# Two instead of four gate tiles inside attention, the six-head run of pooling tiles, and VectorE work queued behind the negated maxima

## The chip, the cores and the metric

The kernel is one program on one core of a Trainium2 chip. The metric is the device time of one execution in microseconds. The engines are named as the profile names them: PE is TensorE (matrix products), with PEld its weight loads; DVE is VectorE, ACT is ScalarE, POOL is GpSimd, SP is SyncE, which here only starts transfers.

## The reference

One decoder layer on 512 tokens of width 1024, in float32:

```python
proj = h @ w_in                       # q | k | v | pool_in | gate_logits
q, k, v, p, g = split(proj)           # 512, 512, 512, 512, 2048 columns
y_attn = moba_attention(q, k, v, rel_bias) @ w_branch_attn   # 8 heads of 64, causal softmax with a bias by distance
y_pool = multiscale_pool(p, w_pool_group, pool_scale) @ w_branch_pool
gates = sigmoid(g).reshape(B, S, 2, D)
mixed = gates[:, :, 0] * y_attn + gates[:, :, 1] * y_pool
h = layer_norm(ALPHA * h + mixed @ w_out)
a, u = split(h @ w_ffn_in)
f = (gelu(causal_dwconv(a)) * u) @ w_ffn_out
h = layer_norm(ALPHA * h + f)
```

With 512 tokens and blocks of 256 the three selected blocks are all the past ones, so attention is plain causal attention. Each head is 512 by 512 scores, of which the lower triangle of 128-wide blocks is computed.

## The kernel before, in words

**Float32 by three products.** A float32 operand is split into a rounded part `hi` and a remainder `lo` (`split`, L71 to L77: ACT writes `hi`, DVE subtracts to get `lo`). A product is three matmuls: hi·hi, hi·lo, lo·hi (`mm3`, lines 243, 246, 247). Every weight slab of 128x1024 thus costs one ACT and one DVE instruction, and sits in a ring of five slots (`slot`); raw slabs land in three buffers (`wraw`, the A slabs of the seven-product form too). `weights(i)` fetches up to `LEAD` = 3 slabs ahead, but not past `state["limit"]`.

**Two ways to make a pair of tiles.** A tile of 128 output channels by 512 tokens and 1024 input channels is either direct (`in_tile`: 8 x 3 matmuls of 512 columns), or two such tiles are made together by a Strassen-like scheme of seven products (`seven`: 7 x 4 x 3 matmuls of 256 columns), with four weight slabs named A, X, D, Y and four forms of the activations (`nT1`, `T3`, `nT2`, `T4`), which `t_form` builds on DVE from the four quarters of x (`quads`) and splits.

**Stages around the change.** First v, the pooling inputs and q and k are made. Then the heads run in a loop of eight. Head h gets its operands by `head` (ACT and DVE cut k and q into parts, and SP copies them to the other half of the partitions: tiles k1, kl, q1), its scores by `scores` (PE; then four DVE instructions that add the bias and take the maxima, `pp` and `nm`; DVE negates the maxima; ACT takes the exponentials with their sums `rs`; DVE inverts; POOL normalizes in four pieces), its transposes by `trans` (ten on PE into three banks `tr`; ACT copies one, DVE two, to `PT`), and two heads at a time their product with v by `pv` (tile `ob`, ACT copies it to `oT`). `head` and `scores` run two heads ahead. As PE's filler between these steps stand tiles that depend on no head: four direct gate tiles (`g0`, `g8`, `g1`, `g9`) in iterations 0 to 3, and in 4 to 7 four pooling tiles `br f, 1` (f = 0 to 3; 4 x 3 matmuls of 512 columns from `zT`, one slab per two tiles), copied by DVE to `gates` (`early_branch`). The four splits of `zT` stand one in each of iterations 0 to 3.

Behind attention come ten more branch tiles (`br 4,1`, `5,1`, `6,1`, and `br f, 0` from `oT` for f = 6 and 0 to 5) with the four forms for the gates between them, and then the gate pairs f = 2 to 7 by `seven` (`sag`, `sbg`, `scg`), the last branch tiles, the output projection (`wo`) and the feed-forward part.

**What sets the order.** The program is recorded in the order of the Python code; a scheduler then puts the instructions of each engine in a fixed order by its own estimated times, and an engine runs its list strictly in that order, waiting at the head of it. `with tc.issue_after(ins):` keeps what is recorded in the block behind `ins` on `ins`'s engine. The output projection and the feed-forward part are the same before and after.

Of the kernel before, what the change touches and what calls it, by code (L numbers as in the profile page):

```python
# [8 lines left out]
F32 = mybir.dt.float32  # L9
# [5 lines left out]
P = 128  # L15
S = 512
# [3 lines left out]
H = 8  # L20
# [18 lines left out]
RAW = 1  # L39
KH = NF // 2  # L40
TAIL = 8
GSEVEN = 2
BRANCH = (("z", 0), ("z", 1), ("z", 2), ("br", 6), ("o", 0), ("o", 1), ("o", 2), ("br", 7))
SEVEN = tuple(range(2, 19))
COVER = 4
# [7 lines left out]
def layer_kernel(ctx: ExitStack, tc: tile.TileContext, xT, x, w_v, w_c, rel_bias, invcnt, w_group,  # L53
                 pscale, w_br, w_out, lnr, w_fi, convp, w_fo, out):
    nc = tc.nc
# [9 lines left out]
    def bank(name):  # L65
        return ps.tile([P, S], F32, tag="ps", name=name)

    def flip(v):
        (pst, pn), (_, n) = v.ap
        return bass.AP(tensor=v.tensor, offset=v.offset + P - 1, ap=[[pst, pn], [P, n // P], [-1, P]])  # L70

    def split(hi, lo, src, copy=None):
        if copy:
            copy(hi, src)
        else:
            state["hi"] = nc.scalar.activation(hi, src, AF.Copy)  # L76
        state["lo"] = nc.vector.tensor_tensor(lo, src, hi.bitcast(F32), op=ALU.subtract)  # L77
        return state["lo"]
# [5 lines left out]
    at = {}  # L84
    pair_of = {}

    def add(key, *tiles):
        at[key] = len(chunks)
        chunks.extend(tiles)

    def add_seven(key, *two):
        pair_of[key] = two
        for q in "AXDY":
            add((*key, q), (key, q))
# [4 lines left out]
    for p in range(pairs):  # L99
        add_seven(("i", 1 + p), w_c[first["q"] + p], w_c[first["k"] + p])  # L100
    fill = [("g", 8 * g + f) for f in range(GSEVEN) for g in range(2)]
    for n, j in fill:
        add((n, j), w_c[first[n] + j])
    for n, key in enumerate(BRANCH[:-1]):
        add(key, w_br[n])
    for f in range(GSEVEN, KT):
        add_seven(("g", f), w_c[first["g"] + f], w_c[first["g"] + KT + f])
    add(BRANCH[-1], w_br[len(BRANCH) - 1])
    WO0 = len(chunks)
# [18 lines left out]
    state = {"next": 0, "limit": WO0 - 1}  # L128
# [107 lines left out]
    def weights(i):  # L236
        while state["next"] <= min(i + LEAD, state["limit"]):
            fetch()
        return ready[i]
# [76 lines left out]
    zT = keepp.enter_context(tc.tile_pool(name="keepz", bufs=1)).tile([P, 4, S], F32, name="zT")  # L316
# [174 lines left out]
    def in_tile(kind, j):  # L491
        wh, wl = split3(weights(at[kind, j]), KT)
        b = bank(f"{kind}{j}")
        for kt in range(KT):
            mm3(b, (wh[:, kt, :], wl[:, kt, :]), (xT_hi[:, kt, :], xT_lo[:, kt, :]), kt == 0, kt == KT - 1)
        if kind == "p":
            return b
        else:
            gslot[j] = gates[:, len(gslot), :]
            nc.scalar.activation(gslot[j], b, AF.Copy)  # L500
# [34 lines left out]
    nms = {}  # L535
    exps = {}
# [65 lines left out]
            scores(0)  # L602
    phase.close()
    keep = keepp.enter_context(tc.tile_pool(name="keep", bufs=1, reuse_waits="tile"))
    gates = keep.tile([P, 2 * GSEVEN + 4, S], F32, name="gates")
    oT = keep.tile([P, 4, S], F32, name="oT")
    zT_hi = keep.tile([P, 4, S], F32R, name="zT_hi")
    zT_lo = keep.tile([P, 4, S], F32R, name="zT_lo")
# [4 lines left out]
    def trans(h):  # L613
        pp = Ps[h]
        PT = ap.tile([P, 10 * P], F32, tag="PT", name=f"PT{h}")
        bk = [bank(f"tr{h}_{n}") for n in range(3)]
        for kb in (0, 1, 3, 2):
            o = toff[kb]
            for i in range(kb, NT):
                c = o + (i - kb) * P  # L620
                nc.tensor.transpose(bk[c // S][:, c % S:c % S + P], pp[:, offs[i] + kb * P:offs[i] + (kb + 1) * P],
                                    ident)
        nc.scalar.activation(PT[:, :S], flip(bk[0]), AF.Copy)
        nc.vector.tensor_copy(PT[:, S:2 * S], flip(bk[1]))
        state["PT"] = nc.vector.tensor_copy(PT[:, 2 * S:], flip(bk[2][:, :2 * P]))
        PTs[h] = PT

    def pv(p):
        b = bank(f"ob{p}")
        for kb in range(NT):  # L630
            n = (NT - kb) * P
            for e in range(2):
                h = 2 * p + e
                state["pv"] = nc.tensor.matmul(b[e * DH:(e + 1) * DH, kb * P:], vv[:, kb, h * DH:(h + 1) * DH],
                                 PTs[h][:, toff[kb]:toff[kb] + n], start=kb == 0, stop=kb == NT - 1)
        state["o"] = nc.scalar.activation(oT[:, p, :], b, AF.Copy)
# [3 lines left out]
    def br_mm(f, br, b=None, ks=range(4), pin=False):  # L640
        key, o = (("br", f), 4 * br) if f >= 6 else (("oz"[br], f // 2), f % 2 * 4)
        wh, wl = split3(weights(at[key]), KT)
        b = b or bank(f"br{f}_{br}")
        for k in ks:
            src = (zT_hi[:, k, :], zT_lo[:, k, :]) if br else (oT_hi[:, k, :], oT_lo[:, k, :])
            mm3(b, (wh[:, o + k, :], wl[:, o + k, :]), src, k == 0, k == 3, pin and k == ks[0])
        return b

    def early_branch(f):
        t = branch[f, 1] = gates[:, 2 * GSEVEN + f, :]  # L650
        nc.vector.tensor_copy(t, br_mm(f, 1))
# [4 lines left out]
    for h in range(H):  # L656
        if h + 2 < H:
            head(h + 2, nms[h], exps[h])
        if h < 4:
            in_tile(*fill.pop(0))  # L660
        elif h < H - 1:
            early_branch(h - 4)
        if h + 2 < H:
            scores(h + 2)
        with ExitStack() as held:
            if h and h % 2 == 0:
                pv(h // 2 - 1)
                held.enter_context(tc.issue_after(state["pv"].ins))
            trans(h)
        if h < 4:  # L670
            with tc.issue_after(nms[h].ins), tc.issue_after(exps[h].ins):
                split(zT_hi[:, h, :], zT_lo[:, h, :], zT[:, h, :])
        if h == 5:
            with tc.issue_after(state["norm"].ins), tc.issue_after(state["dup"].ins):
                for n, (k, t) in enumerate(((k1, t1), (k1, t2), (k2, t1), (k2, t2))):
                    nc.gpsimd.dma_start(quads[n], xT[k.start * P:k.stop * P, t].rearrange("(k p) t -> p k t", p=P))
                homes["g", "X"], homes["g", "D"] = lambda f: gX, lambda f: gD
                for q in "XD":
                    coming[q].remove(("g", GSEVEN))
                    fetch_raw(("g", GSEVEN), q)  # L680
                    homes.pop(("g", q))
        if h == H - 1:
            early_branch(h - 4)
    pv(H // 2 - 1)
    attn.close()

# [4 lines left out]
    more = bp.tile([P, 4, S], F32, name="more")  # L691
# [11 lines left out]
        nc.gpsimd.tensor_tensor(a, b, a, op=ALU.add)  # L703
        mts[f] = a

    unused = [more[:, n, :] for n in range(4)]
    forms = list(parts)
    order = [(4, 1), (5, 1), (6, 1), (6, 0)] + [(f, 0) for f in range(6)]
    for n, (f, br) in enumerate(order):
        if f < GSEVEN:  # L710
            with tc.issue_after(state["o"].ins):
# [35 lines left out]
    for f in range(GSEVEN, KT):  # L747
        if f == KT - 1:
# [3 lines left out]
              lambda ba, u, f=f: gate_done(f, ba, u), first_half if f == KT - 1 else None)  # L752
# [439 lines left out]
```

## Time and profile before

| | |
|---|---|
| time before, median of 3 | 627.69 us (626.48 to 627.84) |
| the profiled execution | 626.34 us, span 624.6 us |
| PE busy | 615.4 us, 99% of the span |
| DVE busy | 513.8 us, 82% |
| ACT busy | 361.6 us, 58% |
| POOL busy | 118.5 us, 19% |
| mean granted PE clock | 0.996 |
| attention loop and branch tiles | about 88 to 181 us of the span |
| gate pairs by seven products | about 181 to 245 us |

Times in rows are microseconds from the start of the span unless marked ns. A busy PE in the profile is not PE at its peak: matmuls are pipelined, so what counts is the distance from one matmul's start to the next one's. In a row of the timeline the second number lasts until the result is written and overlaps the next row.

### The profile page before, as it was taken

The numbers are of one execution on the slowest core, as the hardware profiler recorded it, in microseconds if no ns is written. First come the engines' busy times: TensorE is split into PE (matmuls) and PEld (weight loads), VectorE is DVE, ScalarE is ACT, GpSimd is POOL, SyncE is SP. The second block draws the span as 40 slices with busy tenths as digits, with TensorE's granted clock in tenths as the row PEclk, the third lists the DMA queues.
The fourth block names the chain that finished last, engine by engine and source line by source line (L and its number), as shares of the span: only waits on it lengthen the run. The fifth ranks groups of instructions, "written<-read, shape, count | busy, mean of one in ns | idle before, by whom it ended". The sixth has DMA issues, their size and how long they took to land.

```text
span 624.6 us, 10605 instructions
## 1 busy us (share of the span) xinstructions
PE 615.4 (99%) x4060; PEld 554.8 (89%) x4060; DVE 513.8 (82%) x792; ACT 361.6 (58%) x551; POOL 118.5 (19%) x132
## 2 busy tenths in 40 slices
PE   9999999999999999999999999999999999999995
PEld 6899998786789998889999999999999888888884
DVE  5978788784967988399998988898988959698886
ACT  6746778663756567125566565566656446555452
POOL 0133135344031201110110101101100302123301
PEclk9999999999999999999999999999999999999998
DMA  8566648445486315806658787678744995899805
GB/s 317 165 195 188 172 121 227 124 118 181 123 209 178 103 66 172 301 36 207 164 162 198 200 202 184 176 196 206 186 101 151 331 259 124 204 205 206 204 0 135
DMA packets 41778, 109.29 MB, mean 175 GB/s; under 512 B 4464, under 2 KB 4984, under 8 KB 41472
## 3 DMA queue, kind: packets, MB, share of 16 engines
q1 hardware_dynamic: 27952, 72.55, 34.2%
q0 software_dynamic: 13200, 35.15, 29.3%
q10 hardware_dynamic: 576, 0.92, 0.4%
q8 instruction: 32, 0.52, 0.3%
q14 instruction: 18, 0.15, 0.1%
HBM read 104.39 MB, written 3.17 MB: 172 GB/s over the span
## 4 chain that ended last, share of the span: by engine, by line
PE 97%; DVE 1%; DMA 1%; ACT 0%; POOL 0%; issue 0%; DVEq 0%; POOLq 0%; ACTq 0%
PE saf L243 5%; PE saf L246 5%; PE saf L247 5%; PE v L426 3%; PE fi L243 3%; PE fi L247 3%; PE fi L246 3%; PE sbf L243 3%; PE sbf L247 3%; PE sbf L246 3%; PE wo L246 2%; PE wo L243 2%; PE wo L247 2%; PE br L243 2%; PE br L247 2%; PE br L246 2%
## 5 line engine op out<-in xcount | busy, mean ns | idle before, releaser
L77 DVE TENSOR_TENSOR wlo<-araw,whi 128x1024 fp32r<-128x1024 f32 x56 | 68.1, 1224 | 6.9 <-ACT whi L76 6.4
L76 ACT ACTIVATE whi<-araw 128x1024 fp32r<-128x1024 f32 x56 | 58.7, 1059 | 25.2 <-PE saf L246 5.2
L76 ACT ACTIVATE whi<-wraw 128x1024 fp32r<-128x1024 f32 (+1 forms) x49 | 49.8, 1022 | 35.5 <-DMA wraw<-in_w_fo 8.6
L77 DVE TENSOR_TENSOR wlo<-wraw,whi 128x1024 fp32r<-128x1024 f32 (+1 forms) x49 | 58.4, 1197 | 12.6 <-ACT whi L76 12.4
L76 ACT ACTIVATE whi<-tw 128x1024 fp32r<-128x1024 f32 (+1 forms) x30 | 29.5, 985 | 25.3 <-DMA tw<-in_w_fo 10.5
L190 POOL DMA_DIRECT2D xraw<-in_w_fi x15 | 18.1, 1206 | 134.7 <-DMA xraw<-in_w_fi 74.0
L77 DVE TENSOR_TENSOR wlo<-tw,whi 128x1024 fp32r<-128x1024 f32 (+1 forms) x30 | 33.4, 1129 | 8.5 <-ACT whi L76 8.5
L243 PE MATMUL saf<-hT_hi,whi 128*128 128x256 f32 x136 | 38.0, 279 | 0.0
L243 PE MATMUL sbf<-T_hi,whi 128*128 128x256 f32 x136 | 37.9, 279 | 0.0
L246 PE MATMUL saf<-hT_lo,whi 128*128 128x256 f32 x136 | 37.8, 278 | 0.0
L243 PE MATMUL saf<-nT_hi,whi 128*128 128x256 f32 x136 | 37.8, 278 | 0.0
L247 PE MATMUL saf<-nT_hi,wlo 128*128 128x256 f32 x136 | 37.8, 278 | 0.0
L246 PE MATMUL sbf<-T_lo,whi 128*128 128x256 f32 x136 | 37.7, 278 | 0.0
L247 PE MATMUL sbf<-T_hi,wlo 128*128 128x256 f32 x136 | 37.7, 278 | 0.0
L246 PE MATMUL saf<-nT_lo,whi 128*128 128x256 f32 x136 | 37.7, 277 | 0.0
L247 PE MATMUL saf<-hT_hi,wlo 128*128 128x256 f32 x136 | 37.7, 278 | 0.0
L246 PE MATMUL fi<-hT_lo,whi 128*128 128x256 f32 (+1 forms) x112 | 36.2, 326 | 0.0
L247 PE MATMUL fi<-hT_hi,wlo 128*128 128x256 f32 (+1 forms) x112 | 36.2, 326 | 0.0
L243 PE MATMUL fi<-hT_hi,whi 128*128 128x256 f32 (+1 forms) x112 | 36.1, 327 | 0.0
L566 POOL TENSOR_SCALAR pp<-pp,rs 128x128 f32<-128x128 f32 (+3 forms) x32 | 24.3, 774 | 31.3 <-DVE rs L563 27.8
L231 POOL DMA_DIRECT2D tw<-in_w_fo x18 | 15.6, 901 | 63.0 <-DVE wlo L77 61.4
L243 PEld LDWEIGHTS saf<-hT_hi,whi 128*128 128x128 f32 x136 | 25.5, 188 | 0.1
(356 smaller groups left out, 2207.0 us busy)
## 6 DMA issues: line engine op xcount, KB each, us to landing
tw<-in_w_fo POOLq DMA_DIRECT2D x20, 512.0 KB, 8.6
araw<-in_w_fi SPq DMA_DIRECT2D x17, 512.0 KB, 3.5
xraw<-in_w_fi SPq DMA_DIRECT2D x15, 512.0 KB, 3.9
xraw<-in_w_fi POOLq DMA_DIRECT2D x15, 512.0 KB, 6.5
araw<-in_w_c SPq DMA_DIRECT2D x11, 512.0 KB, 4.1
wraw<-in_w_fi SPq DMA_DIRECT2D x10, 512.0 KB, 3.9
wraw<-in_w_fo SPq DMA_DIRECT2D x10, 512.0 KB, 5.0
tw<-in_w_fo SPq DMA_DIRECT2D x10, 512.0 KB, 6.5
```

The lines of the kernel that those rows point to most:

```text
L76: state["hi"] = nc.scalar.activation(hi, src, AF.Copy)
L77: state["lo"] = nc.vector.tensor_tensor(lo, src, hi.bitcast(F32), op=ALU.subtract)
L190: state["acc"] = nc.gpsimd.dma_start(v, bass.AP(tensor=a.tensor, offset=a.offset, ap=[[pst, pn], [u.offset + S - a.offset, 2], [est, S]]), ...
L231: nc.gpsimd.dma_start(raw, half(then[1:], sl), accum_op=ALU.add)
L243: ins = nc.tensor.matmul(out_, wh, ah, start=start, stop=False, **kw)
L246: nc.tensor.matmul(out_, wh, al, start=False, stop=False, **kw)
L247: nc.tensor.matmul(out_, wl, ah, start=False, stop=stop, **kw)
L426: ins = nc.tensor.matmul(bs[j], xs_[j][a], (wh, wl)[b], start=kt == 0 and n == 0, stop=False)
L566: state["norm"] = nc.gpsimd.tensor_scalar(pp[:, offs[i]:offs[i] + n], pp[:, offs[i]:offs[i] + n], rs[:, i:i + 1], 1.0, op0=ALU.mult, op1=A ...
```

## The change

`GSEVEN` goes from 2 to 1: the direct gate tiles are `g0` and `g8` alone, and the gate pair f = 1 is made by `seven` like f = 2 to 7. The iterations 2 to 7 of the head loop now hold six pooling tiles (f = 0 to 5), so that eight branch tiles are left behind attention instead of ten. Three rules of order are new. The two DVE copies of `trans(h)` stand behind the negated maxima of head h + 2. The four splits of `zT` stand together in iteration 0, on DVE behind the negated maxima of head 2. And the slabs of the branch tiles are fetched by `early_fetch` with a limit that rises by a slab at a time, their splits behind the negated maxima and the exponentials of head h + 1 (of head 7 in the last iteration, where the limit rises to the slab `("o", 1)`, three slabs).

```diff
-GSEVEN = 2
+GSEVEN = 1
...
-    gates = keep.tile([P, 2 * GSEVEN + 4, S], F32, name="gates")
+    gates = keep.tile([P, H, S], F32, name="gates")
...
-        nc.vector.tensor_copy(PT[:, S:2 * S], flip(bk[1]))
-        state["PT"] = nc.vector.tensor_copy(PT[:, 2 * S:], flip(bk[2][:, :2 * P]))
+        with ExitStack() as held:
+            if h + 2 < H:
+                held.enter_context(tc.issue_after(nms[h + 2].ins))
+            nc.vector.tensor_copy(PT[:, S:2 * S], flip(bk[1]))
+            state["PT"] = nc.vector.tensor_copy(PT[:, 2 * S:], flip(bk[2][:, :2 * P]))
...
+    def early_fetch(h, limit):
+        state["limit"] = limit
+        n = min(h + 1, H - 1)
+        with tc.issue_after(nms[n].ins), tc.issue_after(exps[n].ins):
+            weights(limit)
...
-        if h < 4:
+        if fill:
+            state["limit"] = at["z", 0]
             in_tile(*fill.pop(0))
         elif h < H - 1:
-            early_branch(h - 4)
+            early_fetch(h, at["z", 0] + h // 2)
+            early_branch(h - 2 * GSEVEN)
...
-        if h < 4:
-            with tc.issue_after(nms[h].ins), tc.issue_after(exps[h].ins):
-                split(zT_hi[:, h, :], zT_lo[:, h, :], zT[:, h, :])
+        if h == 0:
+            with tc.issue_after(nms[2].ins), tc.issue_after(exps[0].ins):
+                for k in range(4):
+                    split(zT_hi[:, k, :], zT_lo[:, k, :], zT[:, k, :])
...
         if h == H - 1:
-            early_branch(h - 4)
+            early_fetch(h, at["o", 1])
+            early_branch(h - 2 * GSEVEN)
+            state["limit"] = WO0 - 1
...
-    unused = [more[:, n, :] for n in range(4)]
+    unused = [more[:, n, :] for n in range(4)] + [zT[:, 1, :]]
     forms = list(parts)
-    order = [(4, 1), (5, 1), (6, 1), (6, 0)] + [(f, 0) for f in range(6)]
+    order = [(6, 1), (6, 0)] + [(f, 0) for f in range(6)]
```

On DVE, at the last head's softmax: `pp7`, `nm7`, `rs7` belong to head 7, `PT5` and `PT6` are the transposed probabilities of heads 5 and 6, `gates<-br` is the copy of a pooling tile, `wlo` the split of a weight slab. Before:

```order
L555 ISA pp7_1620,nm7_1621<-sc7_3_1625,strip7_1464 128x512
L555 ISA nm7_1621 128x1
L624 COPY PT5_1648<-tr5_1_1650 128x512
L625 COPY PT5_1648<-tr5_2_1651 128x256
L558 TENSOR_SCALAR nm7_1621<-nm7_1621 128x4
L651 COPY gates_1093<-br2_1_1678 128x512
L563 RECIPROCAL rs7_1622<-rs7_1622 128x4
L624 COPY PT6_1702<-tr6_1_1704 128x512
L625 COPY PT6_1702<-tr6_2_1705 128x256
L651 COPY gates_1093<-br3_1_1736 128x512
```

The same place of the changed kernel:

```order
L660 COPY gates_1093<-br4_1_1636 128x512
L558 TENSOR_SCALAR nm7_1579<-nm7_1579 128x4
L627 COPY PT5_1606<-tr5_1_1608 128x512
L628 COPY PT5_1606<-tr5_2_1609 128x256
L563 RECIPROCAL rs7_1580<-rs7_1580 128x4
L627 COPY PT6_1660<-tr6_1_1662 128x512
L628 COPY PT6_1660<-tr6_2_1663 128x256
L77 TENSOR_TENSOR wlo31_1632<-wraw31_1630,whi31_1631 128x1024
L77 TENSOR_TENSOR wlo32_1696<-wraw32_1694,whi32_1695 128x1024
L77 TENSOR_TENSOR wlo33_1702<-wraw33_1700,whi33_1701 128x1024
L660 COPY gates_1093<-br5_1_1706 128x512
```

The negation of head 7's maxima moved ahead of the copies of `PT5`, but the copy of pooling tile 4 now stands directly ahead of it; three slab splits stand behind the copies of `PT6`.

On PE, at the last product with v (`ob3`, heads 6 and 7), where the branch tiles from `oT` begin (`br6_0`, `br0_0` and so on; `br6_1` is the last pooling tile). Before:

```order
L634 MATMUL ob3_1750<-PT6_1702,vv_188 64x128
L634 MATMUL ob3_1750<-PT7_1719,vv_188 64x128
L243 MATMUL br6_1_1832<-zT_hi_1095,whi33_1523 128x512
L246 MATMUL br6_1_1832<-zT_lo_1096,whi33_1523 128x512
L247 MATMUL br6_1_1832<-zT_hi_1095,wlo33_1524 128x512
...
L243 MATMUL br6_0_1849<-oT_hi_1766,whi33_1523 128x512
L243 MATMUL br0_0_1876<-oT_hi_1766,whi34_1673 128x512
```

The same place of the changed kernel:

```order
L247 MATMUL br6_1_1765<-zT_hi_1095,wlo31_1632 128x512
L637 MATMUL ob3_1720<-PT7_1677,vv_188 64x512
L637 MATMUL ob3_1720<-PT6_1660,vv_188 64x384
L637 MATMUL ob3_1720<-PT7_1677,vv_188 64x384
L637 MATMUL ob3_1720<-PT6_1660,vv_188 64x256
L637 MATMUL ob3_1720<-PT7_1677,vv_188 64x256
L637 MATMUL ob3_1720<-PT6_1660,vv_188 64x128
L637 MATMUL ob3_1720<-PT7_1677,vv_188 64x128
L243 MATMUL br6_0_1779<-oT_hi_1736,whi31_1631 128x512
L243 MATMUL br0_0_1806<-oT_hi_1736,whi32_1695 128x512
```

Nine matmuls of `br6_1` stood between the last product with v and the first matmul that reads `oT_hi`; now all twelve stand ahead of that product and none behind it.

## Rows read from the trace of the kernel before

**Rows 1.** The page's chain that ended last: shares of the span by engine.
```profile
PE 97%; DVE 1%; DMA 1%; ACT 0%; POOL 0%; issue 0%; DVEq 0%; POOLq 0%; ACTq 0%
```

**Rows 2.** Busy time by stretch, gate pairs: engines with counts, clock, DMA share, GB/s.
```profile
184.00:230.00 46.00, 46.00 (x401) 46.00 (x400) 38.47 (x49) 26.45 (x42) 8.02 (x7) 1.00 0.45 115
```

**Rows 3.** Timeline of PE: a gate tile, then first gate pair, then output projection.
```profile
119.08 0.39 PE L246 MATMUL g<-xT_lo,whi 128*128 128x512 f32 x1
...
124.31 0.28 PE L551 MATMUL sc<-k,q 128*128 128x256 f32 x1
...
180.84 0.28 PE L243 MATMUL sag<-xT_hi,whi 128*128 128x256 f32 x1
...
244.58 0.39 PE L243 MATMUL wo<-whi,mx_hi 128*128 128x512 f32 x1
```

**Rows 4.** The chain of waits at head 7: start, duration, engine, tile, line.
```profile
138.20 0.23 DVE pp L555
...
138.84 1.14 DVE wlo L77
...
141.06 0.60 DVE PT L624
...
142.00 0.09 DVE nm L558
...
142.17 2.31 ACT pp L561 x8
...
144.85 1.39 POOL pp L566 x3
...
146.29 0.55 PE tr L621 x3
```

**Rows 5.** Timeline of PE from head 7's scores to its first transposes.
```profile
137.55 0.28 PE L552 MATMUL sc<-kl,q 128*128 128x256 f32 x1
...
138.31 1.25 PE L621 MATMUL tr<-ident,pp 128*128 128x128 f32 x10
139.32 0.48 PE L243 MATMUL br<-zT_hi,whi 128*128 128x512 f32 x1
...
142.25 2.37 PE L634 MATMUL ob<-PT,vv 128*64 128x512 f32 x16
144.55 2.28 PE L621 MATMUL tr<-ident,pp 128*128 128x128 f32 x16
146.59 0.48 PE L243 MATMUL br<-zT_hi,whi 128*128 128x512 f32 x1
```

**Rows 6.** Timeline of DVE: a pooling tile's copy, head 6's first score instruction, an inversion.
```profile
129.63 0.69 DVE L651 COPY gates<-br 128x512 f32<-128x512 f32 x1 [0.33 <-PE br L247]
130.24 0.28 DVE L555 CUSTOM_DVE_ANT_0 pp<-sc,strip 128x128 f32<-128x128 f32 x1
...
131.88 0.17 DVE L563 RECIPROCAL rs<-rs 128x4 f32<-128x4 f32 x1
```

**Rows 7.** Timeline of PE: last product with v, and what follows it.
```profile
157.33 2.37 PE L634 MATMUL ob<-PT,vv 128*64 128x512 f32 x14
159.63 0.50 PE L243 MATMUL br<-zT_hi,whi 128*128 128x512 f32 x1
```

**Rows 8.** Timeline of ACT: the copy of that product and its splits.
```profile
159.74 0.60 ACT L636 ACTIVATE oT<-ob 128x512 f32<-128x512 f32 x1 [2.14 <-PE ob L634]
160.23 1.67 ACT L76 ACTIVATE oT_hi<-oT 128x512 fp32r<-128x512 f32 x3
```

**Rows 9.** Transfers of one slab, issued at 120 to 122 and 151.5 to 153: us to landing.
```profile
wraw<-in_w_br SPq DMA_DIRECT2D x1, 512.0 KB, 4.5
...
araw<-in_w_c SPq DMA_DIRECT2D x1, 512.0 KB, 7.6
```

**Rows 10.** Timeline of POOL: the normalization of head 1 and of head 7.
```profile
95.46 4.49 POOL L566 TENSOR_SCALAR pp<-pp,rs 128x128 f32<-128x128 f32 x4 [3.00 <-DVE rs L563]
...
144.85 2.05 POOL L566 TENSOR_SCALAR pp<-pp,rs 128x128 f32<-128x128 f32 x4 [6.57 <-DVE rs L563]
```

## The prediction, made before the changed kernel ran

> **What bounds the kernel now.** I read the chain that ended last first: PE holds 97% of it [rows 1], so a microsecond counts only if it is taken from PE's stream or put into it as a wait. Then the stretches: where the gate pairs run, PE is busy 46.00 of 46.00 us and DVE 38.47 [rows 2], so a pair that is added there costs its matmuls and nothing else, and what shifts this stage's start shifts the end of the program. Then the timeline of PE for the distance between starts, which is what a matmul costs. Last the chain of waits inside attention: it leaves PE at one place, head 7, where it runs over DVE, ACT and POOL back to the transposes [rows 4]. Attention was full of PE filler everywhere else. The change takes away filler, so the question is whether the softmax chains still hide behind what is left.
>
> All sums are made against the profiled execution (626.34 us; span 624.6 and 1.7 around it). The median of the runs is 627.69, 1.35 higher; I add that at the end.
>
> **Term 1, matmuls: -1.21 us.** From the second matmul of a gate tile to the next scores 23 matmuls take 124.31 - 119.08 = 5.23 us, 0.2274 each [rows 3], so a direct gate tile is 24 x 0.2274 = 5.46, and two of them are 10.92. The stretch from the first gate pair to the output projection, 244.58 - 180.84 = 63.74 us, holds six pairs and two branch tiles of 12 matmuls (5.46): (63.74 - 5.46) / 6 = 9.71 per pair [rows 3]. The number of pooling and branch tiles stays at fourteen. So 9.71 - 10.92 = -1.21. The new pair's four slabs, its sums and its transfers lie in the stage of [rows 2], where DVE has 16% to spare.
>
> **Term 2, head 7's softmax: +1.24 us.** I set a clock to 0 at the second part of head 7's scores (the products with kl), 137.55 before [rows 5].
>
> DVE: the first of the four score instructions starts at 138.20, 0.65 later [rows 4]. The four take 131.88 - 130.24 = 1.64 when nothing stands between them [rows 6], so they end at 2.29. Before, a slab split of 1.14 stood between and the copies of PT5 behind, from 141.06 to 142.00, 0.94 [rows 4]; both are out of the way now. But the copy of pooling tile 4 stands there: 0.61 (129.63 to 130.24 [rows 6]), and it needs the tile's last matmul. PE reaches that at 0.76 for the scores (137.55 to 138.31 [rows 5]) plus five matmuls of 0.23, 1.9, so the copy waits for nothing and ends at 2.90, and the negation begins there. From the negation (142.00) to the exponentials (142.17) are 0.17, from these to the transposes that the third normalized piece frees 146.29 - 142.17 = 4.12 [rows 4]. Those transposes can run at 2.90 + 0.17 + 4.12 = 7.19.
>
> PE: behind the five matmuls stand only the product with v of heads 4 and 5 (144.55 - 142.25 = 2.30) and ten transposes (139.32 - 138.31 = 1.01 [rows 5]): 1.92 + 2.30 + 1.01 = 5.23, and three transposes of head 7 that need the first pieces, 0.30: PE stands ready at 5.53 and waits 1.66. Before, a whole pooling tile lay in between, and 16 transposes took 146.59 - 144.55 = 2.04 against 16 x 0.101 = 1.62: a wait of 0.42 [rows 5]. The difference is +1.24. Part of it will show earlier, inside the product with v: its fourth matmul reads a copy of PT5 that ends only at about 3.7. It is the same delay, not a second one.
>
> [...]
>
> **Term 3, the cover behind the last product with v: +1.2 us.** The change puts all twelve matmuls of `br6_1` ahead of that product, and the next matmuls read `oT_hi`. Before, PE ended the product at 159.63 [rows 7], ACT began the copy at 159.74, the splits at 160.23, three of them in 1.67, 0.56 each [rows 8]: the first `oT_hi` was there at 160.79, 1.16 after the product, and nine matmuls (2.05) hid it. Now nothing does: 1.16 and a handoff, 1.2. It can't be less while the order stands.
>
> **Term 4, the A slab of the new pair on ACT: +0.4 us.** ACT's list has the splits of two slabs (`whi34`, `whi35`) ahead of that copy, and `whi35` is the pair's first slab. Before, the A slab of the first pair was fetched before head 7. Now it waits for one of the three raw buffers, which the three slab splits behind PT6 free one by one (the second of them frees this one). On the clock above: the inversion of head 7 at 3.07 + 2.33 = 5.4 (144.50 by the chain's 2.31 of exponentials), copies of PT6 0.94, then splits of 1.14 [rows 4]: buffers come free at about 7.7 and 8.8. A slab takes 4.5 us to land where little else moves and took 7.6 while the four blocks of x were in flight [rows 9]; here they start at about 7.9, so I take the 7.6. It lands at 13.3 to 16.4, `whi35` is done at 14.3 to 17.4. PE ends the last product with v at about 16.7 (7.19 + 0.3, tile 5 at 2.75, four transposes 0.4, one matmul of about 0.9, tile 6 at 2.75, and 2.30 [rows 7]). So 0 to 0.7, and `oT_lo` stands on DVE behind the first of the four forms of x; I take 0.4. If the transfers took 10 us it would be 3.
>
> **Edits at nothing.** The negated maxima of heads 2 to 6 ahead of the copies to PT: PE had no wait there, so nothing is won, and the copies' readers, the products with v, still come behind a pooling tile; by the durations above I estimate the thinnest cover at 0.5 (heads 2 and 3); a pooling tile's copy late in front of them would cost 0.1 (0.61 less 0.5). The splits of zT: four at 0.6 on DVE, done while PE is still in gate tile `g8`, ahead of pooling tile 0. The three slab splits ahead of the copies of PT7: 3 x 1.14 after 6.5 ends at 9.9, before those transposes. The four forms lose two branch tiles of cover, 5.46. From 17.4 on DVE's list has nine splits and forms at 1.14 and eight instructions of half that size at 0.6 up to the pair's second slab, 32.5; PE asks for it at 16.7 + 1.6 + 84 x 0.2274 + 24 x 0.116 = 40.2. If the blocks of x held DVE up for over 7.7 us, that cover would be gone.
>
> Sum: -1.21 + 1.24 + 1.2 + 0.4 = +1.63. Profiled time 627.97; on the median 629.3.
>
> [...] POOL's normalization took 2.05 us for head 7, when DVE did little, and 4.49 for head 1, when DVE ran slab and zT splits beside it [rows 10]. In the changed order a slab split stands behind the copies of PT6, at about 6.5, just as POOL begins its third piece at 6.6.
> [...]
>
> **Rivals.**
> - *The waits don't come (faster), 626.1.* DVE and ACT are through earlier than my clock says, and PE is dense as before: -1.21 - 0.42 = -1.63 on the median. For it: heads 3 to 6 had no wait at the same kind of filler. Against it: term 3 is a chain of two ACT instructions behind one PE instruction, with nothing between on PE. It decides if tile 4's copy or PT5 is not in the way and `oT` comes out in under half a microsecond.
> - *One gap only (no change), 627.7.* Head 7's chain costs no more than the 0.42 of before and the A slab lands in time: -1.21 + 1.2 = 0. For it: before, the chain also hid nearly all but this. Against it: a pooling tile less in front of it.
> [...]
>
> **Chances.** My forecast 0.47, with an own range of 628.2 to 630.6; waits don't come 0.13; one gap 0.26; choke 0.14. Within 0.2% (1.26 us, about what a measurement of this kernel can tell) I count the one-gap case and a fifth of my own, 0.35; slower 0.38 + 0.14 = 0.52; faster 0.13. The range leaves out half of the fast case and a tail of the slow one: 626.3 to 631.3.
>
> **What would show it.** Right: in the changed profile PE's transposes of head 7 wait for POOL by over a microsecond, PE is idle for 1.2 us or more between the last product with v and the first `oT_hi` matmul, and the gate pairs take 9.7 us each, seven of them, in an unbroken stream. The output projection starts 1.6 us later than at 244.58. Wrong: a gap between those two under 0.5 us, a copy of PT5 that comes before the last matmul of tile 4, an A slab landed before the last product with v by several microseconds (term 4 gone), or waits in heads 2 to 6, where I count none.

## The result, and the profile after

| | before | after |
|---|---|---|
| median of 6 runs each | 626.92 us (626.29 to 627.84) | 630.88 us (630.29 to 633.98) |
| profiled execution, its span | 626.34, 624.6 us | 631.48, 629.8 us |

The ratio is 1.0069, 95% interval 1.0047 to 1.0091: slower by 4.0 us in the medians and 4.3 by the ratio, where 629.3 against 627.69 was forecast, 1.6. The direction was right, the loss 2.4 to 2.7 us too small in the forecast.

The chain that ended last, in the page of the changed kernel, has lost 3% of PE to a transfer and to DVE [rows 1]:

```profile
PE 94%; DMA 3%; DVE 2%; issue 1%; ACT 0%; DVEq 0%; ACTq 0%
```

The timeline of PE, from head 7's scores to the output projection, answers to [rows 3, 5, 7]:

```profile
134.75 0.28 PE L552 MATMUL sc<-kl,q 128*128 128x256 f32 x1
...
136.75 3.22 PE L637 MATMUL ob<-PT,vv 128*64 128x512 f32 x16
139.90 2.67 PE L621 MATMUL tr<-ident,pp 128*128 128x128 f32 x16
142.33 0.48 PE L243 MATMUL br<-zT_hi,whi 128*128 128x512 f32 x1
...
149.65 2.37 PE L637 MATMUL ob<-PT,vv 128*64 128x512 f32 x14
154.74 3.22 PE L243 MATMUL br<-oT_hi,whi 128*128 128x512 f32 x7 [2.72 <-ACT oT_hi L76]
157.75 0.63 PE L246 MATMUL br<-oT_lo,whi 128*128 128x512 f32 x1
...
175.52 0.28 PE L243 MATMUL sag<-xT_hi,whi 128*128 128x256 f32 x1
...
248.96 0.39 PE L243 MATMUL wo<-whi,mx_hi 128*128 128x512 f32 x1
```

Four distances between starts carry the account. The product of heads 4 and 5 takes 139.90 - 136.75 = 3.15, of which 2.30 are matmuls. The sixteen transposes take 142.33 - 139.90 = 2.43, of which 1.62 are matmuls. Together PE waits 1.66 at head 7. The last product ends 2.30 after 149.65, at 151.95, and the first matmul with `oT_hi` starts at 154.74: a gap of 2.79. The 84 matmuls from there to the first gate pair take 175.52 - 154.74 = 20.78 instead of 84 x 0.2267 = 19.04 (run 12 below has them in 19.04): 1.74 too long. The seven pairs and two tiles take 248.96 - 175.52 = 73.44, just 7 x 9.71 + 5.46. So -1.21 + (1.66 - 0.42) + 2.79 + 1.74 = +4.56, and the output projection starts 248.96 - 244.58 = 4.38 later; 0.2 stays unassigned.

What made the gap of 2.79 is seen in the chain of waits of the changed kernel (start, duration, what):

```profile
143.63 1.22 DVE wlo L77
...
144.87 7.73 DMA araw<-in_w_c
...
152.62 0.02 ACT whi L76
...
153.59 0.58 ACT oT L639
154.17 0.53 ACT oT_hi L76
```

A raw buffer comes free when DVE ends a slab split at 144.85. The A slab of the new pair is issued into it and takes 7.73 to land. Its split stands ahead of the copy of `oT` on ACT, so the copy starts at 153.59, though its product had ended at 151.95.

Why the buffer came free no earlier is seen in the timelines of DVE and of POOL:

```profile
141.03 0.69 DVE L627 COPY PT<-tr 128x512 f32<-128x512 f32 x1 [0.62 <-PE tr L621]
...
141.97 1.74 DVE L77 TENSOR_TENSOR wlo<-wraw,whi 128x1024 fp32r<-128x1024 f32 x1
```

```profile
140.58 2.06 POOL L566 TENSOR_SCALAR pp<-pp,rs 128x128 f32<-128x128 f32 x4 [7.31 <-PE tr L621]
```

The copies of PT6 waited 0.62 for head 6's transposes, which stand on PE behind the product of heads 4 and 5 and its wait for PT5. Then the first slab split took 1.74, beside POOL's last piece (141.95 to 142.64); the two splits behind it took 1.21 each.

What made the 1.74 is seen in the windows of the changed kernel (busy time of PE, PEld, DVE, ACT, POOL, then granted clock, DMA share, GB/s) and in DVE's timeline:

```profile
152.00:154.70 2.70, 0.01 (x1) 0.00 (x0) 0.99 (x1) 2.08 (x4) 0.00 (x0) 1.00 1.03 354
154.70:158.40 3.70, 3.66 (x9) 2.90 (x10) 3.70 (x6) 3.68 (x6) 0.00 (x0) 0.54 1.03 258
```

```profile
153.71 1.23 DVE L77 TENSOR_TENSOR wlo<-araw,whi 128x1024 fp32r<-128x1024 f32 x1 [3.40 <-ACT whi L76]
154.86 1.22 DVE L264 TENSOR_TENSOR quad<-quad,quad 128x1024 f32<-128x1024 f32 x1
155.99 1.89 DVE L77 TENSOR_TENSOR oT_lo<-oT,oT_hi 128x512 fp32r<-128x512 f32 x3
```

After PE had been idle for 2.72, the granted clock was 0.54 of full speed over 3.7 us (154.70 to 158.40): seven matmuls took 157.75 - 154.74 = 3.01, 0.43 each instead of 0.227. And `oT_lo` came only at 156.6, behind the A slab's lower split and a form of x. One of the two, or both, made the 1.74; the filler below tells them apart.

Behind the output projection the profiled execution loses another 0.8 of its span (629.8 - 248.96 against 624.6 - 244.58) in the feed-forward part, which is the same code. A wait of 0.18 at 337.06 is part of it; the rest stays open. This execution is 0.6 above the median of its kernel.

### The profile page after: what moved, and what is told of

Same layout as the page of the kernel before. It is cut to its first block, busy times and chain, and to the rows that moved or that the text cites. A ratio compares the mean times of both kernels' runs of the same rounds, so it can differ in the third digit from the quotient of the medians.

```text
span 629.8 us, 10684 instructions
## 1 busy us (share of the span) xinstructions
PE 617.5 (98%) x4096; PEld 557.2 (88%) x4096; DVE 517.7 (82%) x801; ACT 362.5 (58%) x553; POOL 119.2 (19%) x133
## 4 chain that ended last, share of the span: by engine, by line
PE 94%; DMA 3%; DVE 2%; issue 1%; ACT 0%; DVEq 0%; ACTq 0%
PE saf L243 5%; PE saf L247 5%; PE saf L246 5%; PE v L426 3%; PE fi L243 3%; PE fi L247 3%; PE fi L246 3%; PE wo L247 2%; PE wo L246 2%; PE wo L243 2%; PE sbf L247 2%; PE br L243 2%; PE sbf L243 2%; PE sbf L246 2%; PE sag L243 2%; PE br L246 2%
## 5 line engine op out<-in xcount | busy, mean ns | idle before, releaser
L77 DVE TENSOR_TENSOR wlo<-araw,whi 128x1024 fp32r<-128x1024 f32 x58 | 70.6, 1225 | 12.7 <-ACT whi L76 12.1
L76 ACT ACTIVATE whi<-araw 128x1024 fp32r<-128x1024 f32 x58 | 60.8, 1058 | 26.7 <-PE saf L246 5.3
L77 DVE TENSOR_TENSOR wlo<-wraw,whi 128x1024 fp32r<-128x1024 f32 (+1 forms) x47 | 56.0, 1201 | 13.4 <-ACT whi L76 13.2
L76 ACT ACTIVATE whi<-wraw 128x1024 fp32r<-128x1024 f32 (+1 forms) x47 | 47.3, 1017 | 31.8 <-DMA wraw<-in_w_fo 8.1
L243 PEld LDWEIGHTS saf<-nT_hi,whi 128*128 128x128 f32 x136 | 25.5, 188 | 0.5 <-ACT fT L297 0.4
```

The costliest lines, as they stand in the source:

```text
L243: ins = nc.tensor.matmul(out_, wh, ah, start=start, stop=False, **kw)
```

## The experiments

Each run has a ratio to the kernel before, timed beside it. The intervals of runs 1 to 4 overlap that of the changed kernel, so their times alone don't tell them from it; what each edit did is read from the trace. The profiled execution shows the mechanism, and it can stand some microseconds off its kernel's median: 3.2 above in run 4, 2.7 below in run 7. An edit also moves other instructions, because the scheduler orders the lists anew.

**1. The A slab behind `oT_hi`.**

```diff
         split(oT_hi[:, k, :], oT_lo[:, k, :], oT[:, k, :])
+        if k == 2:
+            late = [state["hi"].ins, state["lo"].ins]
...
+        with ExitStack() as held:
+            for ins in late:
+                held.enter_context(tc.issue_after(ins))
+            weights(at["br", 6] if f >= 6 else at["oz"[br], f // 2])
         b = br_mm(f, br)
```

> The changed kernel, but the last slab of attention and the A slab of the new pair are split behind oT_hi instead of ahead of the copy of oT. Theory (the late A slab holds oT up, and the wait of 2.79 us lets TensorE's clock fall): the wait shrinks to oT copy plus first split, 1.1 to 1.2 us, -1.6; if 1.2 us of idle leaves the clock up, another -1.7: 3.3 less than the changed kernel, 0.7 above the kernel before. Rival 1 (the clock falls after a wait of a microsecond too): -1.6 only, 2.4 above before. Rival 2 (term 3 alone, the missing cover, and the slab is not what holds oT): no change, 4.0 above before.

Measured: 630.39 us, ratio 1.0067 (1.0045 to 1.0089). PE's timeline:

```profile
149.63 2.37 PE L637 MATMUL ob<-PT,vv 128*64 128x512 f32 x14
153.20 0.97 PE L243 MATMUL br<-oT_hi,whi 128*128 128x512 f32 x3 [1.21 <-ACT oT_hi L76]
...
172.38 0.28 PE L243 MATMUL sag<-xT_hi,whi 128*128 128x256 f32 x1
...
180.99 0.39 PE L243 MATMUL sbg<-gT_hi,whi 128*128 128x256 f32 x1 [1.51 <-ACT quad L295]
...
247.62 0.39 PE L243 MATMUL wo<-whi,mx_hi 128*128 128x512 f32 x1
```

The theory holds up to the first gate pair: the wait is 1.21, the clock in the next 3.7 us is 1.00, and the pair starts 175.52 - 172.38 = 3.14 earlier. (The edit puts the slab's lower split behind `oT_lo` too, so it takes away both possible causes of the 1.74.) But the time did not follow: 4.2 above before by the ratio, where 0.7 was forecast. At 180.99 stands a new wait of 1.51, and the stage takes 247.62 - 172.38 = 75.24, 1.8 more than in the changed kernel. The chain there names its cause:

```profile
169.55 9.96 DMA quad<-in_w_c
```

This is the second transfer of the X slab of the second gate pair (the one that adds), into the buffer of a block of x, which is free only when that block's form is split. In the changed kernel it was issued 0.8 earlier, at 168.73, and had landed by 177.8, some 3 us before PE would have had to wait for it. Here it lands at 179.5, and PE is there 3.1 earlier. My sum of what the edit would give had no such bound in it, and that was wrong.

**2. The cover alone.** Nine matmuls of `br6_1` go back behind the last product.

```diff
...
         for k in ks:
+            if behind and k == 1:
+                held.enter_context(tc.issue_after(behind))
...
-        b = br_mm(f, br)
+        b = br_mm(f, br, behind=None if n else state["pv"].ins)
```

> The changed kernel with nine of the twelve matmuls of br6_1 put back behind the last product with v, as before. Theory: the product ends 2 us earlier, but oT stands behind whi35 on ACT, which waits for the A slab, so the first oT_hi matmul starts at the same place (20.0 us behind head 7's second part of scores) and nothing is won: 4.0 above before, PE idle 2.5 to 2.8 us ahead of oT_hi, the clock falls again. Rival (term 3: the cover is what is missing): 1.2 to 2.0 less than the changed kernel, 2 to 2.8 above before.

Measured: 631.1 us, ratio 1.0066 (1.005 to 1.0083), no gain.

```profile
147.77 2.37 PE L637 MATMUL ob<-PT,vv 128*64 128x512 f32 x14
154.93 1.65 PE L243 MATMUL br<-oT_hi,whi 128*128 128x512 f32 x4 [2.50 <-ACT oT_hi L76]
```

The product starts 1.9 earlier and `oT_hi` comes when it came before. The granted clock behind the wait is 0.60 from 154.70 to 158.40. The cover that term 3 missed was not what ended last; the A slab was.

**3. The negation ahead of tile 4's copy.**

```diff
-        nc.vector.tensor_copy(t, br_mm(f, 1))
+        b = br_mm(f, 1)
+        with ExitStack() as held:
+            if f == 4:
+                held.enter_context(tc.issue_after(nms[H - 1].ins))
+            nc.vector.tensor_copy(t, b)
```

> The changed kernel with the negation of head 7's maxima ahead of the copy of pooling tile 4 on DVE. Theory (term 2): the chain of head 7 begins 0.6 us earlier, PE's wait there falls from 1.66 to 1.05, and since the slab splits stand behind head 7's exponentials on ACT, the A slab comes as much earlier: 0.6 less than the changed kernel, 3.4 above before. Rival (the slab's landing doesn't follow head 7): the wait only moves to the place ahead of oT_hi, 4.0 above before.

Measured: 629.86 us, ratio 1.0046 (1.0033 to 1.006). PE's timeline:

```profile
137.06 2.75 PE L637 MATMUL ob<-PT,vv 128*64 128x512 f32 x16
139.74 2.67 PE L621 MATMUL tr<-ident,pp 128*128 128x128 f32 x16
142.17 0.48 PE L243 MATMUL br<-zT_hi,whi 128*128 128x512 f32 x1
```

(139.74 - 137.06 - 2.30) + (142.17 - 139.74 - 1.62) = 1.19 of wait instead of 1.66. The wait ahead of `oT_hi` fell too, to 1.72: on head 7's clock DVE starts its split of the A slab at 17.51 (152.58 - 135.07) instead of 18.96 (153.71 - 134.75). This time the clock stayed up:

```profile
154.70:158.40 3.70, 3.59 (x16) 2.65 (x15) 2.88 (x6) 3.68 (x6) 0.00 (x0) 1.00 1.07 269
```

Of the 0.6 that I put on tile 4's copy in term 2, 0.5 was there. How much of the 1.0 in the medians is the edit's is not shown: the transfer and the clock may differ between executions, and this one, 628.72, is the fastest of its six.

**4. A filler instead of the idle time.** Eleven matmuls on PE where it stood idle.

```diff
         b = br_mm(f, br)
+        if n == 0:
+            dull = bank("dull")
+            with tc.issue_after(state["pv"].ins):
+                for _ in range(11):
+                    nc.tensor.matmul(dull, zT_hi[:, 0, :P], zT_hi[:, 1, :], start=True, stop=True)
```

> The changed kernel with eleven matmuls of 512 columns (2.5 us), whose result nobody reads, put on PE behind the last product with v, where it stood idle for 2.79 us. Nothing else moves. Theory (the idle stretch lets the clock fall, and the nine matmuls behind it took 0.43 instead of 0.227 us each for that reason): the granted clock stays at 1.00, oT_hi starts at the same place, and the matmuls behind it run at 0.227: 1.7 less than the changed kernel, 2.3 above before. Rival (these matmuls were slow because oT_lo was late or because the transfers were at their highest then): no change, 4.0 above before.

Measured: 630.18 us, ratio 1.0052 (1.0037 to 1.0066), 3.3 above before where my theory had 2.3. Its profiled execution came to this place 2.4 us late, so only distances are compared:

```profile
152.04 2.37 PE L637 MATMUL ob<-PT,vv 128*64 128x512 f32 x14
...
154.34 2.79 PE L733 MATMUL dull<-zT_hi 128*128 128x512 f32 x11
157.24 1.65 PE L243 MATMUL br<-oT_hi,whi 128*128 128x512 f32 x6
159.24 0.50 PE L246 MATMUL br<-oT_lo,whi 128*128 128x512 f32 x1 [0.34 <-DVE oT_lo L77]
...
177.09 0.28 PE L243 MATMUL sag<-xT_hi,whi 128*128 128x256 f32 x1
```

With PE busy the clock stays at 1.00 behind the place (154.70 to 162.00), so the idle time is what let it fall. But the 84 matmuls still take 177.09 - 157.24 = 19.85, 0.81 over the 19.04: at full speed PE runs into `oT_lo`. Of the 1.74, then, 0.9 is the clock's own, and 0.8 is `oT_lo`, behind which the slow matmuls hid. Both my theory (all of it the clock) and the rival were half right.

**5 and 6. Each half of the change undone.** First the tile counts of before with the new orders (the line with `h // 2` then reaches one slab further ahead, since the pooling tiles start two iterations later), then two gate tiles with the orders of before (the splits of `zT` stay together in iteration 0).

```diff
-GSEVEN = 1
+GSEVEN = 2
...
-    order = [(6, 1), (6, 0)] + [(f, 0) for f in range(6)]
+    order = [(4, 1), (5, 1), (6, 1), (6, 0)] + [(f, 0) for f in range(6)]
```

> The changed kernel with two features still formed as direct gate tiles in attention (four gate tiles, the first pooling tile at head 4, two pooling tiles behind attention), as in the kernel before, but with the new orders on DVE and the weights one tile ahead. Theory (what costs is the missing cover behind attention, not the orders): the A slab comes behind oT on ACT, pooling tiles 4 and 5 stand between the last product with v and oT_hi, no wait over 0.5 us there: 0 from the kernel before, -0.5 to +0.6. Rival (the weights one tile ahead come too late wherever they stand): a wait of 1.5 to 3 us for a slab behind attention, 2 to 4 above before.

```diff
-            if h + 2 < H:
-                held.enter_context(tc.issue_after(nms[h + 2].ins))
...
-            state["limit"] = at["z", 0]
...
-            early_fetch(h, at["z", 0] + h // 2)
...
-            early_fetch(h, at["o", 1])
```

> The changed kernel with two gate tiles in attention, but the weights three slabs ahead and the copies to PT in the order of before (no negation put ahead). Theory: the A slab is fetched before head 7's chain and its split stands ahead of PT7, so the wait behind the last product with v is the 1.1 to 1.2 of term 3, the clock stays up, and head 7 waits 1.5 to 2.5: 1 to 2.5 above before, so less than the changed kernel's 4.0. Rival (the missing cover costs the same whichever order the slabs have): 4 above before or more.

Measured: 628.0 us, ratio 1.0023 (1.0015 to 1.0032), and 627.97 us, ratio 1.0020 (1.0010 to 1.0029). Each half costs some 1.3 us, both together 4.3; for the first the theory had 0. The first shows no wait ahead of `oT_hi`, as the theory had it, but one at head 7 that I had not counted: the product of heads 4 and 5 takes 146.26 - 142.65 = 3.61 there instead of 2.30, and the sixteen transposes 148.68 - 146.26 = 2.42 instead of 1.62. So the new orders are not free even with four gate tiles. The second, PE's timeline:

```profile
132.81 0.36 PE L552 MATMUL sc<-kl,q 128*128 128x256 f32 x1
...
137.17 2.38 PE L635 MATMUL ob<-PT,vv 128*64 128x512 f32 x16
139.47 2.15 PE L621 MATMUL tr<-ident,pp 128*128 128x128 f32 x16
141.38 0.48 PE L243 MATMUL br<-zT_hi,whi 128*128 128x512 f32 x1
...
148.75 2.37 PE L635 MATMUL ob<-PT,vv 128*64 128x512 f32 x14
152.33 0.97 PE L243 MATMUL br<-oT_hi,whi 128*128 128x512 f32 x3 [1.21 <-ACT oT_hi L76]
```

The wait ahead of `oT_hi` is term 3's 1.2, with nothing on top. Head 7 waits 141.38 - 139.47 - 1.62 = 0.29, as little as before and not the 1.5 to 2.5 that I expected. From head 7's kl products to the product of heads 4 and 5 PE now has 137.17 - 132.81 = 4.36 us of work, where the changed kernel has 2.00: with the slabs fetched earlier the scheduler puts all twelve matmuls of tile 4 behind the scores, not five.

**7. All three repairs at once** (edits 1, 2 and 3 together).

> The changed kernel with the slab splits behind oT_hi, nine matmuls of br6_1 behind the last product with v, and the negation ahead of tile 4's copy. Theory (after the run with the slab alone, where the gate stage took back 1.8 us: the X slab of the second gate pair lands at 179.5, and PE had to wait 1.5 us for it): no wait ahead of oT_hi, the first gate pair starts at 170.7, but the second pair's X slab comes at 179 as before and PE waits about 2.7 there: the output projection starts at 247.1, 2.2 to 3 above before. Rival (each wait taken away is won in full): 3.1 + 1.2 + 0.5 less than the changed kernel, 0.9 below before.

Measured: 633.84 us, ratio 1.0114 (1.0098 to 1.0129): slower than the changed kernel. PE's timeline, then the window behind:

```profile
180.82 0.39 PE L243 MATMUL sbg<-gT_hi,whi 128*128 128x256 f32 x1 [3.04 <-ACT quad L295]
...
249.03 0.39 PE L243 MATMUL wo<-whi,mx_hi 128*128 128x512 f32 x1
```

```profile
181.00:185.00 4.00, 4.00 (x25) 4.00 (x25) 2.06 (x3) 0.98 (x4) 0.00 (x0) 0.66 1.03 244
```

The first pair starts at 170.67 (170.7 was expected), and the wait ends at 180.82, as late as in run 1 (180.99). The wait of 3.04 then costs twice, since the clock falls to 0.66 over the 4 us behind it: the stage takes 249.03 - 170.67 = 78.36 instead of 73.44, 1.9 more than the wait. That second price I had left out again. With both, this execution is only as late at the output projection as the changed kernel (248.96); it is the fastest of its five, and what the others lose beyond it is not shown.

**8. The X slab in a buffer of its own.** The kernel of 7, with

```diff
-                homes["g", "X"] = lambda f: (gX, qraw[1], qraw[3])[(f - GSEVEN) % 3]
+                gX2 = zT[:, 2:4, :].rearrange("p a t -> p (a t)")
+                homes["g", "X"] = lambda f: gX2 if f == 2 else (gX, qraw[1], qraw[3])[(f - GSEVEN) % 3]
```

> The kernel with all three edits, and the second gate pair's X slab in two rows of zT that nobody reads after its splits, instead of the buffer of the second block of x, so that it is fetched during attention. Theory (X of the second pair was what took the gain back): PE runs through from oT_hi to the output projection, whose start comes 4.4 to 4.9 earlier than in the changed kernel, 244.1 to 244.6: 0.9 below before, -0.2 to -1.2. Rival (another transfer of the gate stage is as late, or the earlier fetch holds the strips and POOL up in attention): 1 us or more of waits elsewhere, 0.5 to 2.5 above before.

Measured: 627.64 us, ratio 1.0009 (0.9998 to 1.002): no difference from before that can be told, 6 us less than 7, and not the 0.9 below before that I expected. The wait for X is gone, so X was the bound. What is left is smaller: a wait of 0.75 in the first pair (175.61, for ACT's copy to zT), and 1.0 in the feed-forward part of this execution.

**9 and 10. Which of the two rules.** The change with the weights three slabs ahead again (the fetch lines of 6 undone, the negation's rule kept), and the reverse (only the negation's rule undone).

> The changed kernel with the weights three slabs ahead, as in the kernel before; the negation stays ahead of the copies to PT. Theory (of the two rules it is the fetch one tile ahead that costs, since it makes the A slab late): as with both rules undone, a wait of 1.2 ahead of oT_hi at full clock, the output projection at 244.5 to 245.1: 0.3 to 1.2 above before. Rival (the negation's rule costs too, or it is the one): 2 to 4 above before.

> The changed kernel without the rule that puts the negation ahead of the copies to PT; the weights stay one tile ahead. DVE's and ACT's lists then have the split of the A slab ahead of the copies of PT7. Theory (the late A slab is what costs, and whatever stands behind its split waits for it): the slab lands at 17 to 18 us on head 7's clock, the copies of PT7 and with them fourteen matmuls of the last product with v come behind it, and the wait moves from oT_hi to that product and grows: 5 to 7 above before. Rival (undoing either rule is enough): 1 above before. Rival 2 (the negation's rule is worth nothing here): 4 above before, as the changed kernel.

Measured: 628.0 us, ratio 1.0029 (1.0018 to 1.004), with a wait of 1.21 ahead of `oT_hi` and 0.24 at head 7; and 636.63 us, ratio 1.016 (1.0146 to 1.0173). Without the fetch rule 1.8 us of loss are left by the ratio (0.3 to 1.2 was expected), and undoing the negation's rule as well (run 6) makes no difference that can be told. So the fetch one tile ahead costs some 2.5 of the 4.3, and with the slabs three ahead the negation's rule gives and takes nothing. The profiled executions of runs 6 and 9 reach the output projection 0.5 and 1.1 later than before (245.03 and 245.64); the rest of their loss stays open. With the late fetch the negation's rule is needed: without it the loss is ten microseconds, more than I expected and at another place. PE's timeline of run 10, DVE's, and POOL's:

```profile
145.91 0.47 PE L621 MATMUL tr<-ident,pp 128*128 128x128 f32 x1 [2.37 <-POOL pp L566]
```

```profile
139.73 0.29 DVE L555 CUSTOM_DVE_ANT_0 pp<-sc,strip 128x128 f32<-128x128 f32 x1 [0.96 <-PE sc L552]
...
146.08 3.96 DVE L77 TENSOR_TENSOR wlo<-wraw,whi 128x1024 fp32r<-128x1024 f32 x3 [0.77 <-ACT whi L76]
```

```profile
145.48 5.03 POOL L566 TENSOR_SCALAR pp<-pp,rs 128x128 f32<-128x128 f32 x4 [9.12 <-DVE rs L563]
```

PE's list now has all of tile 4 and two matmuls of the product ahead of head 7's kl products, so DVE gets its first scores only at 139.73, and little is left to hide the softmax: the transposes wait 2.37 for POOL and then 0.83 more. The granted clock is 0.55 from 145 to 150 and 0.76 from 150 to 155, so the matmuls behind the wait are slow too: seven of 512 columns take 152.00 - 149.01 = 2.99, 0.43 each. My reason, the A slab ahead of PT7's copies, was not it: no wait stands ahead of the last product at 157.63.

**11 and 12. The loss taken out.** Two gate tiles with the orders of before, head 7's last transposes ahead of `br6_1`, its matmuls six and six around the last product, the last slab splits behind the copies of PT7 (11); and `oT_lo` ahead of the A slab's lower split and the second form (12).

```diff
...
+            if behind and k in (0, 2):
+                held.enter_context(tc.issue_after(behind[k // 2]))
...
+        with ExitStack() as held:
+            for ins in state["copies"]:
+                held.enter_context(tc.issue_after(ins))
+            weights(at["br", 6] if f >= 6 else at["oz"[br], f // 2])
-        b = br_mm(f, br)
+        b = br_mm(f, br, behind=() if n else (state["tr"].ins, state["pv"].ins))
```

> The changed kernel with both rules undone (weights three slabs ahead, no negation put ahead), head 7's last four transposes ahead of br6_1, six matmuls of br6_1 behind them and six behind the last product with v, and the last two slab splits behind the copies of PT7. Theory (terms 1 and 3: what is left of the loss is the 1.2 of missing cover, and 1.36 us of matmuls hide it): no wait over 0.4 ahead of oT_hi, the output projection at 243.6 to 244.2, 0.4 to 1 earlier than in the kernel before: 0.3 above to 0.8 below before. Rival (the six matmuls are missed where they were, ahead of the last product with v, whose copies of PT7 then end too late): a wait of 0.8 or more there, no gain over both rules undone, 1.1 above before.

```diff
+        if k == 2:
+            late = state["lo"].ins
...
-            for ins in state["copies"]:
+            for ins in state["copies"] + ((late,) if f < GSEVEN else ()):
...
-            with tc.issue_after(state["PT"].ins):
+            with tc.issue_after(state["PT"].ins if n == 1 else late):
```

> The kernel of v3_cover with the first three oT_lo ahead of the A slab's lower split and of the second form of x on DVE. There the wait had moved from oT_hi to oT_lo: 1.22 us at 154.28, while DVE did a slab split and a form first. Theory (DVE's list only has to give oT_lo in time; its other work has cover): that wait is gone, 0.3 or less, the output projection starts 1.2 earlier than in v3_cover, at 244.1, 0.5 before the kernel before: 0.3 to 0.9 below before, and the whole -1.21 of term 1 less what head 7 keeps shows. Rival (the forms pushed behind make the gate stage late, as in the run with the slab behind oT_hi): a wait of 0.5 to 1.5 at the second gate pair, no gain, 0.5 above before.

Measured: 627.04 us, ratio 1.0008 (0.9996 to 1.0021), and 625.72 us, ratio 0.9985 (0.9974 to 0.9997). In 11 the wait only moved, from `oT_hi` to `oT_lo`, and the output projection did not start earlier than before, though I had expected that. PE's timeline of 11, then of 12:

```profile
151.29 1.77 PE L243 MATMUL br<-oT_hi,whi 128*128 128x512 f32 x7
154.28 0.50 PE L246 MATMUL br<-oT_lo,whi 128*128 128x512 f32 x1 [1.22 <-DVE oT_lo L77]
```

```profile
150.88 1.75 PE L243 MATMUL br<-oT_hi,whi 128*128 128x512 f32 x7
152.46 0.39 PE L246 MATMUL br<-oT_lo,whi 128*128 128x512 f32 x1
...
169.92 0.28 PE L243 MATMUL sag<-xT_hi,whi 128*128 128x256 f32 x1
...
243.36 0.39 PE L243 MATMUL wo<-whi,mx_hi 128*128 128x512 f32 x1
```

In 12 PE runs through. The 84 matmuls take 169.92 - 150.88 = 19.04, and the output projection starts 244.58 - 243.36 = 1.22 earlier than in the kernel before: term 1, alone at last. This version is ahead of both kernels, of the one before by 0.15% (0.03 to 0.26%).

## Why the prediction was right, point by point

- *The forecast as a whole: right, in part by luck.* The measured 630.88 lies inside the stated 626.3 to 631.3, but above the 628.2 to 630.6 of my own case: the range reached so far up for the sake of the choke in the chances, which did not come true. And the forecast stood on a median before of 627.69, which six runs put at 626.92. It had 1.6 of loss where 4.0 to 4.3 was measured, and more than half of that lies in what term 4 sized too small and in what no term held.
- *Term 1, -1.21: right.* The pairs run at 9.71 each in an unbroken stream, and kernel 12 shows the term by itself, 1.22.
- *Term 2, +1.24: the size right, its cause within the change wrong.* The clock gave 7.19 for the transposes and 1.66 of wait; 1.66 was measured. I put it to a pooling tile less in front of head 7. Runs 6 and 9 have no more tiles there and wait 0.29 and 0.24. With the slabs three ahead the scheduler leaves twelve and nine matmuls behind the scores instead of five, and puts tile 4's copy behind the negation instead of ahead of it. Run 3 gives the copy 0.5; four matmuls more are 0.9 by an estimate from [rows 3]; together that is the difference to run 9. Of the sign that I named, a wait of over a microsecond for POOL at head 7's transposes, only 0.81 is there; the other 0.85 stands in the product, which waits for PT5.
- *Term 3, +1.2: right, but hidden behind term 4.* 1.21 shows in runs 1, 6 and 9, where no slab stands in the way. In the changed kernel giving the cover back won nothing (run 2).
- *Term 4, +0.4: the step that was mis-sized.* The gap of 2.79 is 1.2 of term 3 and 1.6 of the A slab. The transfer took what I had taken, 7.73 for 7.6. It was issued late: at 10.1 on head 7's clock (144.87 - 134.75), where I had 8.8. My slab splits started at 6.5 and ran at 1.14; they started at 7.2 (141.97), and two of them lasted until 10.1. I had counted the late PT5 on PE alone; it also held up head 6's transposes, and with them the copies of PT6 on DVE, 0.6. And the first split took 0.5 longer beside POOL. So `whi35` was done at 18.8 (153.59), past the bound of 17.4.
- *What no term held: 1.74 behind the gap.* I had noted that `oT_lo` stands behind a form, and gave it nothing (0.8 by run 4). That a wait of this length, 2.72, is followed by a lower clock (0.54 over 3.7 us, which cost 0.9) was in none of my cases. Terms 4 and this together are 3.3 where the forecast has 0.4; that is nearly the whole error.
- *POOL beside the slab splits.* Head 7's normalization took 2.06 in the changed kernel, as in [rows 10]: the split did not hold it up. In run 10 three slab splits ran beside it from 146.08, and it took 5.03. In the changed kernel the two met as well, and there it was the split that took longer: 1.74 instead of 1.21, beside POOL's last piece, which took 0.69 from 141.95, as its last piece did before. No run shows what decides which of the two takes longer.
- *Edits at nothing.* Heads 2 to 6 and the splits of zT cost nothing on PE. The forms' cover, which I put at 7.7, was not the tight one: the X slab behind the forms was, with some 3 us to spare, as runs 1, 7 and 8 show.
- *Rivals.* The choke has 0.14 of the chances and sets the upper end of the range, but the changed kernel shows no loss on POOL to stand behind it: there the split took 0.5 longer, POOL 2.06 as before, and the A slab 7.73 to land, against the 7.6 of term 4.

## What to carry to other kernels

Where an engine runs an ordered list, price a late transfer by its issue: go back to the instruction that frees its buffer, and count everything that stands behind its first reader. After taking a wait away, look for the transfer that lands next: here three repairs, two of which showed what they should on PE, were together slower than none until that transfer was moved too. And a wait of TensorE as long as those of 2.4 to 3.0 us here is to be priced twice, for itself and for the clock behind it (0.54 to 0.66 in the 3.7 to 4 us behind three of them).

## What was not expected of the hardware

The granted clock behind a wait of PE on its critical path: behind 1.21 and 1.51 (run 1) and 1.72 (run 3) it stayed at 1.00; behind 2.72 (the changed kernel), 2.50 (run 2) and 3.04 (run 7) it was 0.54 to 0.66 over the next 3.7 to 4 us, and behind 2.37 (run 10), with a second wait of 0.83 close by, 0.55 from 145 to 150 and 0.76 from 150 to 155. With useless matmuls in the place of the idle time it stayed at 1.00 (run 4). The adding transfer of an X slab, 512 KB, took 9.96 to land in run 1 and 9.0 in the changed kernel (issued at 168.73); a plain one of that size took 9.0 in run 1, issued 0.8 behind it, and 5.6 in the changed kernel, issued 0.1 behind it. So no run here shows what the adding itself costs, nor what made the difference between the plain ones.
